# Leaving out the query columns of the first 10 or 14 tokens in eight attention-like heads

## The chip, the cores and the metric

The kernel runs on one core of one Trainium2 chip. The metric is device time in microseconds (us) of one execution; lower is better. TensorE (PE), VectorE (DVE), ScalarE (ACT), GpSimd (POOL) and SyncE (SP) each run their own list of instructions in order and wait for each other by semaphores.

## The reference, cut to what matters

The input is 1024 frames of 1024 features in float32; 16 learned meta tokens are put ahead of them (T = 1040 tokens). A token mixer with four mLSTM ("gated") heads and four retention heads is followed by a gated feed-forward network with a causal convolution over 3 tokens, and a final norm.

```
proj = up @ w_in                                   # up: normalised tokens
qk = silu(causal_dwconv(concat([ml_q, ml_k]), ml_conv_w))   # 4 taps, gated heads
rq = rotary(rt_q, pos); rk = rotary(rt_k, pos)              # retention heads
h = h + concat([gate(o) * head_norm(mlstm(q, k, v)), silu(g) * head_norm(retention(rq, rk, rv))]) @ w_out
h = h + channel_mixer(rmsnorm(h))     # its convolution takes the 2 tokens before each token
return rmsnorm(h)[:, 16:]             # the meta tokens are dropped at the end
```

Each token's query is used for that token's output alone. Only tokens 16 and later are returned, and the feed-forward convolution takes two tokens before them, so the mixer's output is needed from token 14 on. Keys and values of all tokens are needed, since they go into the running state.

## The kernel before, in words

Each matrix product in float32 is three TensorE products of rounded halves: high by high (L404), high by low (L405), low by high (L406). The queries and the keys of one head are a matrix of 128 rows (features) by 1040 columns (tokens), built in the three pieces of `PIECES`: columns 0 to 400, 400 to 784 and 784 to 1040. A piece is 8 blocks of the 1024 input features by three products, 24 matmuls, into one PSUM bank (`pq` for queries, `pk` for keys). `KEEP = 14` is the first token whose mixer output is needed; the output gate's first piece (`po`, 386 columns) starts there already, the query's starts at 0.

A piece is then taken out of PSUM. In a gated head (h = 0 to 3) DVE scales it (L425), copies three columns of overlap (L423), and runs the four taps of the convolution (L428 and three of L430) into `cvq` or `cvk`; ACT applies silu (L431) into `qT` or `kT`. In a retention head (h = 4 to 7) four DVE operations (L433 to L436) apply the rotary embedding and write `qT` or `kT`; ACT has no part in it. `qT` and `kT` are one tile each, used by all heads in turn.

The heads go in the order `ORDER = [4, 0, 1, 2, 3, 5, 6, 7]`. While one head's chunks are scanned (`scan_a`: scores `s` L816, weighted keys `kwh` on ACT L829; then the state update `u` on PE, L846), the matmuls of the next projections are laid between them. After a head's last chunk come its statistics (root L911 on ACT, L914 and L915 on DVE, the scaling L918 on ACT). `exps` (L555 to L559) makes the decay weights of a gated head: POOL adds a mask, ACT takes nine exponentials. `L808` and L809 split a scaled query into its halves on ACT and DVE. `L162` and L163 split weights into halves.

ACT holds one set of function tables at a time. Silu, sigmoid (L447), root and exponential change it, and the compiler puts an `ACT_TABLE_LOAD` before an activation that needs another set; it has the line of that activation. POOL also issues the accumulating DMAs of `w_out` (L212). The order of each engine's list comes from a scheduler of the framework, which runs a simulated timeline; so an edit may move instructions elsewhere.

Of the kernel before, what the change touches and what calls it, by code (L numbers as in the profile page):

```python
# [23 lines left out]
KEEP = 14  # L24
H = 4
# [38 lines left out]
def body(ctx, tc, h_in, vecs, cst, mask_in, rot, w_v0, w_v, w_fm, w_out, w_up, w_gate, w_down, out):  # L64
    nc = tc.nc
# [45 lines left out]
    def pp(name, tag="pp"):  # L111
        return ps.tile([P, 512], F32, tag=tag, name=name, bufs=PSB[tag])
# [58 lines left out]
    def need(key, ahead, loads=0):  # L171
        if not order:
            order.update({u[0]: i for i, u in enumerate(units)})
        issue(order[key] + 1 + ahead)
        if loads:
            load(order[key] + 1 + loads)
        return ready[key]
# [178 lines left out]
    qT = st.tile([P, T], F32, name="qT", tag="qT")  # L356
# [42 lines left out]
    def fm_mms(pt, U, t0, t1):  # L399
        hi, lo, _ = U  # L400
        n = t1 - t0
        for kb in range(KB):
            a, b = hi[:, kb * P:(kb + 1) * P], lo[:, kb * P:(kb + 1) * P]
            nc.tensor.matmul(pt[:, :n], a, uh[kb][:, t0:t1], start=kb == 0, stop=False)  # L404
            nc.tensor.matmul(pt[:, :n], a, ul[kb][:, t0:t1], start=False, stop=False)  # L405
            nc.tensor.matmul(pt[:, :n], b, uh[kb][:, t0:t1], start=False, stop=kb == KB - 1)  # L406
# [2 lines left out]

    def qk_group(h, kind, p):  # L410
        t0, t1, _ = PIECES[p]
        n = t1 - t0
        U = need((kind, h, 0), 2)
        pt = pp(f"p{kind}{h}_{p}")
        fm_mms(pt, U, t0, t1)
        dst = (qT if kind == "q" else kT)[:, t0:t1]
        raw = wk.tile([P, WMAX + 4], F32, tag="rawp", name=f"r{kind}{h}_{p}", bufs=2)
        if h < H:
            if p == 0:
                nc.vector.memset(raw[:, :3], 0.0)  # L420
            else:
                pr, pn = halo[kind]
                nc.vector.tensor_copy(raw[:, :3], pr[:, pn:pn + 3])  # L423
            halo[kind] = (raw, n)
            last["qk"] = nc.vector.tensor_tensor(raw[:, 3:3 + n], pt[:, :n], Rb[:, t0:t1], ALU.mult)  # L425
            w = V_CONV + ((0 if kind == "q" else H) + h) * 4
            cv = wk.tile([P, WMAX], F32, tag="cv", name=f"cv{kind}{h}_{p}", bufs=2)
            nc.vector.tensor_scalar(cv[:, :n], raw[:, 3:3 + n], vec[:, w + 3:w + 4], None, ALU.mult)  # L428
            for j in (2, 1, 0):
                nc.vector.scalar_tensor_tensor(cv[:, :n], raw[:, j:j + n], vec[:, w + j:w + j + 1], cv[:, :n], ALU.mult, ALU.add)  # L430
            last["silu"] = nc.scalar.activation(dst, cv[:, :n], AF.Silu)  # L431
        else:
            nc.vector.tensor_tensor(raw[0:64, :n], pt[64:128, :n], A2[64:128, t0:t1], ALU.mult)  # L433
            nc.vector.tensor_tensor(raw[64:128, :n], pt[0:64, :n], A2[0:64, t0:t1], ALU.mult)
            last["qk"] = nc.vector.tensor_tensor(dst, pt[:, :n], A1[:, t0:t1], ALU.mult)
            nc.vector.tensor_tensor(dst, dst, raw[:, :n], ALU.add)  # L436

    def o_group(h, b, p):
        t0, t1, _ = PIECES[p]
        t0 = max(t0, KEEP)  # L440
        n = t1 - t0
        U = need(("o", h, b), 4 if b and p and h not in (HF, 7) else 2)
        pt = pp(f"po{h}_{b}_{p}")
        fm_mms(pt, U, t0, t1)
        s = sig(b, p)
        nc.vector.tensor_tensor(s, pt[:, :n], Rb[:, t0:t1], ALU.mult)
        x = nc.scalar.activation(s, s, AF.Sigmoid if h < H else AF.Silu)  # L447
        if h < H:
            after(x, last["silu"])
        last["gate"] = x  # L450
# [564 lines left out]
    for kind in "qk":  # L1015
        for p in range(3):
            qk_group(HF, kind, p)
# [10 lines left out]
    for i, h in enumerate(ORDER):  # L1028
        A = lambda c, h=h: (lambda: scan_a(h, c))
        B = lambda c, h=h: ab(h, c)  # L1030
        merge([lambda b=b, p=p: (o_group(h, b, p), p == 1 and b and i and wsum_next()) for b in range(2) for p in range(3)],
              [A(0)] + [B(c) for c in range(4 if h < 7 else NCH)])
        if h == 7:
            break
        side = post_steps(h, 0) + [B(4), B(5), B(6)] + post_steps(h, 1) + [B(7), B(8)] + post_steps(h, 2)
        nxt = ORDER[i + 1]
        merge([lambda c=c: (v_group(nxt, c)(), c == 4 and i == 4 and wsum_next()) for c in range(NCH)], side)
        if i:
            tables(nxt)
        else:  # L1040
            exps(nxt)
        for kind in "qk":
            for p in range(3):
                qk_group(nxt, kind, p)
# [612 lines left out]
```

## Time and profile before

| what | value |
|---|---|
| time, median of 3 runs | 1535.11 us (1534.65 to 1535.12) |
| the profiled execution, its own time | 1536.01 us |
| its span, first to last instruction | 1534.2 us |
| mean granted TensorE clock | 0.997 of full speed |
| PE busy | 1516.1 us (99%) |
| DVE busy | 1094.6 us (71%) |
| ACT busy | 723.4 us (47%) |
| POOL busy | 101.5 us (7%) |

The profiled execution took 0.9 us more than the median of the runs, and 1.8 us of its time lie outside the span of instructions. A busy share is an average over the whole span; times of single instructions below are in us from the span's start.

### The profile page before, as it was taken

Reading aid. Unit: us, or ns where it says so; the run is one execution under the profiler, and the core shown is the slowest. Engines: PE = TensorE matmul, PEld = TensorE weight load, DVE = VectorE, ACT = ScalarE, POOL = GpSimd, SP = SyncE. Lnnn points to the kernel's source line nnn. Section 1 sums busy time; section 2 is a strip of 40 time slices with the busy share of each in tenths; the row PEclk is TensorE's granted clock in tenths of the full one; section 3 lists DMA queues with packets and bytes.
Section 4 is the critical chain, followed back from the end, with each engine's and each line's share of the span. In section 5 each row is a group of like instructions: output and inputs, shape, how many; then the busy total and the mean of one; then the engine's idle time right before and its main releaser. Section 6 shows DMA issues by size and latency. Waiting matters only on the chain.

```text
span 1534.2 us, 25396 instructions
## 1 busy us (share of the span) xinstructions
PE 1516.1 (99%) x9749; PEld 1392.2 (91%) x9749; DVE 1094.6 (71%) x2342; ACT 723.4 (47%) x1484; POOL 101.5 (7%) x120
## 2 busy tenths in 40 slices
PE   8999999999999999999999999999999999999997
PEld 7999999999999999997788998999999999888887
DVE  8767667676867575679968878667666666778657
ACT  7365554555542434335455455444444444344443
POOL 0000001010010000000000000211111010000000
PEclk9999999999999999999999999999999999999999
DMA  6123435352566334446443237888666667933313
GB/s 230 56 70 94 107 90 124 118 121 88 143 142 158 80 104 89 111 100 237 178 138 110 83 121 247 209 211 204 159 154 153 151 153 210 357 109 103 96 42 110
DMA packets 106232, 213.41 MB, mean 139 GB/s; under 512 B 10424, under 2 KB 32640, under 8 KB 106112
## 3 DMA queue, kind: packets, MB, share of 16 engines
q1 hardware_dynamic: 87424, 176.86, 34.8%
q0 software_dynamic: 18544, 34.87, 15.1%
q8 instruction: 76, 1.25, 0.3%
q14 instruction: 44, 0.36, 0.1%
q10 hardware_dynamic: 144, 0.07, 0.0%
HBM read 182.37 MB, written 84.19 MB: 174 GB/s over the span
## 4 chain that ended last, share of the span: by engine, by line
PE 97%; DVE 1%; ACT 1%; DMA 0%; issue 0%; DVEq 0%; ACTq 0%
PE pv L394 4%; PE pv L395 4%; PE pv L396 4%; PE po L404 4%; PE po L406 4%; PE po L405 4%; PE pdx L577 3%; PE pdx L579 3%; PE pdx L578 3%; PE pup_x L578 2%; PE pup_x L579 2%; PE pup_x L577 2%; PE pga_x L577 2%; PE pga_x L579 2%; PE pga_x L578 2%; PE pq L404 2%
## 5 line engine op out<-in xcount | busy, mean ns | idle before, releaser
L394 PE MATMUL pv<-hi_v,uh 128*128 128x256 f32 (+1 forms) x512 | 147.0, 288 | 2.6 <-ACT hi_v L162 1.6
L395 PE MATMUL pv<-lo_v,uh 128*128 128x256 f32 (+1 forms) x512 | 145.2, 284 | 0.0
L396 PE MATMUL pv<-hi_v,ul 128*128 128x256 f32 (+1 forms) x512 | 145.1, 284 | 0.0
L404 PE MATMUL po<-uh,hi_o 128*128 128x386 f32 (+2 forms) x384 | 124.0, 323 | 0.0
L405 PE MATMUL po<-ul,hi_o 128*128 128x386 f32 (+2 forms) x384 | 122.6, 319 | 0.0
L406 PE MATMUL po<-uh,lo_o 128*128 128x386 f32 (+2 forms) x384 | 122.6, 319 | 0.0
L394 PEld LDWEIGHTS pv<-hi_v,uh 128*128 128x128 f32 x512 | 97.3, 190 | 6.3 <-issue 2.9
L395 PEld LDWEIGHTS pv<-lo_v,uh 128*128 128x128 f32 x512 | 97.1, 190 | 0.9 <-DVE lo_v L163 0.8
L396 PEld LDWEIGHTS pv<-hi_v,ul 128*128 128x128 f32 x512 | 97.0, 190 | 0.0
L261 ACT CAST hi_up<-raw_up 128x512 fp32r<-128x512 f32 (+1 forms) x52 | 36.4, 719 | 110.0 <-PE pga_z L578 61.2
L212 POOL DMA_DIRECT2D wsd<-w_down_d x55 | 50.9, 1022 | 497.2 <-DMA wsd<-w_down_d 398.1
L404 PEld LDWEIGHTS po<-uh,hi_o 128*128 128x128 f32 x384 | 72.4, 189 | 0.2
L406 PEld LDWEIGHTS po<-uh,lo_o 128*128 128x128 f32 x384 | 72.3, 188 | 0.1
L405 PEld LDWEIGHTS po<-ul,hi_o 128*128 128x128 f32 x384 | 72.3, 188 | 0.1
L262 DVE TENSOR_TENSOR lo_ga<-fraw_ga,hi_ga 128x512 fp32r<-128x512 f32 (+1 forms) x52 | 41.9, 810 | 42.6 <-ACT hi_ga L261 42.5
L262 DVE TENSOR_TENSOR lo_up<-raw_up,hi_up 128x512 fp32r<-128x512 f32 (+1 forms) x52 | 41.4, 810 | 37.1 <-ACT hi_up L261 36.3
L577 PE MATMUL pup_x<-uh_g,hi_up 128*128 128x256 f32 (+1 forms) x240 | 67.3, 282 | 0.4 <-ACT uh_g L1061 0.4
L578 PE MATMUL pup_x<-ul_g,hi_up 128*128 128x256 f32 (+1 forms) x240 | 67.4, 282 | 0.1
L579 PE MATMUL pup_x<-uh_g,lo_up 128*128 128x256 f32 (+1 forms) x240 | 66.4, 282 | 0.0
L212 POOL DMA_DIRECT2D wsw<-w_out_d x40 | 37.2, 1028 | 398.7 <-DMA wsw<-w_out_d 361.4
L404 PE MATMUL pq<-uh,hi_q 128*128 128x400 f32 (+2 forms) x192 | 62.6, 326 | 0.2 <-DVE rq L425 0.2
L405 PE MATMUL pk<-ul,hi_k 128*128 128x400 f32 (+2 forms) x192 | 62.2, 324 | 0.0
(761 smaller groups left out, 5044.8 us busy)
## 6 DMA issues: line engine op xcount, KB each, us to landing
raw_up<-w_up_d SPq DMA_DIRECT2D x22, 512.0 KB, 5.6
fraw_ga<-w_gate_d SPq DMA_DIRECT2D x22, 512.0 KB, 3.7
acts<-cv SPq DMA_DIRECT2D x44, 256.0 KB, 6.1
wsd<-w_down_d SPq DMA_DIRECT2D x22, 512.0 KB, 6.8
wsd<-w_down_d POOLq DMA_DIRECT2D x22, 512.0 KB, 6.5
rd<-wsd SPq DMA_DIRECT2D x22, 512.0 KB, 3.6
wsd<-w_down_d POOLq DMA_DIRECT2D x33, 256.0 KB, 6.9
raw_o<-w_fm_d SPq DMA_DIRECT2D x16, 512.0 KB, 3.5
```

The costliest lines, as they stand in the source:

```text
L212: nc.gpsimd.dma_start(x, v, accum_op=ALU.add)
L261: nc.scalar.copy(hi[:, o:o + n], x)
L262: nc.vector.tensor_tensor(lo[:, o:o + n], x, hi[:, o:o + n].bitcast(F32), ALU.subtract)
L394: nc.tensor.matmul(pv[:L, :nv], a, hi[:, o:o + nv], start=kb == 0, stop=False)
L395: nc.tensor.matmul(pv[:L, :nv], a, lo[:, o:o + nv], start=False, stop=False)
L396: nc.tensor.matmul(pv[:L, :nv], b, hi[:, o:o + nv], start=False, stop=kb == KB - 1)
L404: nc.tensor.matmul(pt[:, :n], a, uh[kb][:, t0:t1], start=kb == 0, stop=False)
L405: nc.tensor.matmul(pt[:, :n], a, ul[kb][:, t0:t1], start=False, stop=False)
L406: nc.tensor.matmul(pt[:, :n], b, uh[kb][:, t0:t1], start=False, stop=kb == KB - 1)
L577: m.append(nc.tensor.matmul(pt, ah, xh_, start=first and k == 0, stop=False, skip_group_check=True))
L578: nc.tensor.matmul(pt, ah, xl_, start=False, stop=False, skip_group_check=True)
L579: m.append(nc.tensor.matmul(pt, al, xh_, start=False, stop=last and k == n - 1, skip_group_check=True))
```

## The change

In the first piece of the queries the product starts at column 10 in gated heads and at column 14 in retention heads. The columns before are no longer computed in any step of that piece (matmul, scaling, convolution, silu or rotary). One GpSimd copy for each head fills columns 0 to 10 (or 14) of `qT` from the columns that start at 14. A gated head keeps four columns more than are needed, of which the convolution reads three.

```
     def qk_group(h, kind, p):
         t0, t1, _ = PIECES[p]
+        cut = kind == "q" and p == 0
+        if cut:
+            t0 = KEEP - (4 if h < H else 0)
         n = t1 - t0
         U = need((kind, h, 0), 2)
         pt = pp(f"p{kind}{h}_{p}")
...
             last["qk"] = nc.vector.tensor_tensor(dst, pt[:, :n], A1[:, t0:t1], ALU.mult)
             nc.vector.tensor_tensor(dst, dst, raw[:, :n], ALU.add)
+        if cut:
+            nc.gpsimd.tensor_copy(qT[:, :t0], qT[:, KEEP:KEEP + t0])
```

In the changed file the lines of the projection's evacuation stand 3 further down (silu is L434), the copy is L441, and everything behind it is 5 further down (the root is L916, the split of a scaled query L813).

ACT, at the first query piece of head 1, before; `num` is the previous head's numerator, `cvq` the convolved query, `z` the statistics, `A` the decay weights:

```order
L880 COPY num_2_2682<-n_8_2732 128x257 [waits PE_49]
L431 ACT_TABLE_LOAD
L431 ACTIVATE qT<-cvq_0_2843 128x400 [waits DVE_49]
L911 ACT_TABLE_LOAD
L911 ACTIVATE z_2_2743<-z_2_2743 128x2 [waits DVE_49]
L559 ACT_TABLE_LOAD
```

The same place in the changed kernel:

```order
L885 COPY num_2_2684<-n_8_2734 128x257 [waits PE_49]
L434 ACT_TABLE_LOAD [waits DVE_49]
L434 ACTIVATE qT<-cvq_0_2845 128x390 [waits Pool_49]
L916 ACT_TABLE_LOAD
L916 ACTIVATE z_2_2745<-z_2_2745 128x2 [waits DVE_49]
L564 ACT_TABLE_LOAD
```

The order of the rows is the same. The silu now waits for POOL as well, since an earlier copy of POOL has read columns of `qT` that it overwrites, and the wait for DVE now stands on the table load ahead of it. Heads 0, 2 and 3 show the same.

PE, behind the last matmul of head 4's first query piece, before; `pra` and `pca` are small products for the norm factors of the tokens:

```order
L325 MATMUL pra_594<-cs,Rc 128x128 x2
L314 MATMUL pca_622<-cs,ssa_609 128x1 [waits Activation_49]
L314 MATMUL pca_622<-cs,ssa_609 128x1
L404 MATMUL pq_1_681<-uh_78,hi_q_0_399 128x384 [waits DVE_49]
L405 MATMUL pq_1_681<-ul_79,hi_q_0_399 128x384
```

In the changed kernel the same two products stand here:

```order
L404 MATMUL pq_1_682<-uh_80,hi_q_0_399 128x384
L405 MATMUL pq_1_682<-ul_81,hi_q_0_399 128x384
L314 MATMUL pca_622<-cs,ssa_609 128x1 [waits Activation_49]
L314 MATMUL pca_622<-cs,ssa_609 128x1
L406 MATMUL pq_1_682<-uh_80,lo_q_0_400 128x384
```

They have moved behind the first 11 matmuls of the second query piece.

DVE, at head 2's second query piece, before; `rq` is the scaled query, `qd` a query times its decay:

```order
L833 TENSOR_TENSOR qd_1_4207<-qT,A_190 128x128 [waits DMAHW4_49,Activation_49]
L425 TENSOR_TENSOR rq_1_3949<-pq_1_3924,Rb 128x384 [waits PE_49]
L914 RECIPROCAL z_2_3818<-z_2_3818 128x2 [waits Activation_49]
L428 TENSOR_SCALAR cvq_1_3952<-rq_1_3949,vec 128x384 [waits DVE_49]
L423 COPY rq_2_3983<-rq_1_3949 128x3
```

The same place in the changed kernel:

```order
L838 TENSOR_TENSOR qd_1_4211<-qT,A_190 128x128 [waits DMAHW4_49,Activation_49]
L919 RECIPROCAL z_2_3821<-z_2_3821 128x2 [waits Activation_49]
L428 TENSOR_TENSOR rq_1_3953<-pq_1_3928,Rb 128x384 [waits PE_49]
L920 SCALAR_TENSOR_TENSOR mv_2_3761<-mv_2_3761,z_2_3821 128x2 [waits DVE_49]
L431 TENSOR_SCALAR cvq_1_3956<-rq_1_3953,vec 128x384 [waits DVE_49]
```

The reciprocal, which waits for the root on ACT, now stands ahead of the scaling that empties the PSUM bank of the second piece. Heads 1 and 3 show the same.

## Rows read from the trace of the kernel before

**Rows 1.** The page: busy time by engine; the chain that ended last, by engine.

```profile
PE 1516.1 (99%) x9749; PEld 1392.2 (91%) x9749; DVE 1094.6 (71%) x2342; ACT 723.4 (47%) x1484; POOL 101.5 (7%) x120
...
PE 97%; DVE 1%; ACT 1%; DMA 0%; issue 0%; DVEq 0%; ACTq 0%
```

**Rows 2.** PE's waits: who waits for whom, us in total, times, longest.

```profile
PE pv L394 <- ACT hi_v L162: 1.6, 1, 1.6
...
PE pca L314 <- ACT Rb L329: 0.9, 2, 0.6
```

**Rows 3.** Timeline of PE, first query pieces: start, us, instruction, [idle before <- releaser].

```profile
39.17 0.34 PE L404 MATMUL pq<-uh,hi_q 128*128 128x400 f32 x1
...
42.80 0.34 PE L406 MATMUL pq<-uh,lo_q 128*128 128x400 f32 x1
...
46.69 0.34 PE L405 MATMUL pq<-ul,hi_q 128*128 128x384 f32 x1
...
50.54 0.34 PE L406 MATMUL pq<-uh,lo_q 128*128 128x384 f32 x1
```

**Rows 4.** Timeline of ACT, head 1, from the first query piece on.

```profile
220.76 1.28 ACT L431 ACT_TABLE_LOAD   x1
222.32 0.54 ACT L431 ACTIVATE qT<-cvq 128x400 f32<-128x400 f32 x1 [0.27 <-DVE cvq L430]
...
232.21 0.28 ACT L808 CAST qd_2h<-qd 128x128 fp32r<-128x128 f32 x1
...
247.66 0.42 ACT L431 ACTIVATE kT<-cvk 128x256 f32<-128x256 f32 x1 [0.39 <-DVE cvk L430]
248.08 1.28 ACT L447 ACT_TABLE_LOAD   x1
249.37 0.94 ACT L447 ACTIVATE sig<-sig 128x386 f32<-128x386 f32 x2
250.22 0.35 ACT L829 ACTIVATE kwh<-s,cols 128x128 fp32r<-128x128 f32 x1
```

**Rows 5.** Timeline of DVE, the same stretch.

```profile
221.65 0.63 DVE L430 SCALAR_TENSOR_TENSOR cvq<-rq,vec,cvq 128x400 f32<-128x400 f32 x1
...
228.56 0.29 DVE L809 TENSOR_TENSOR qd_1l<-qd,qd_1h 128x128 fp32r<-128x128 f32 x1 [1.44 <-ACT qd_1h L808]
...
232.52 0.29 DVE L809 TENSOR_TENSOR qd_2l<-qd,qd_2h 128x128 fp32r<-128x128 f32 x1 [0.40 <-ACT qd_2h L808]
...
247.13 0.48 DVE L430 SCALAR_TENSOR_TENSOR cvk<-rk,vec,cvk 128x256 f32<-128x256 f32 x1
```

**Rows 6.** Timeline of PE, head 1's first state update.

```profile
250.62 0.39 PE L846 MATMUL u<-vh,kwh 128*128 128x258 f32 x1
```

**Rows 7.** Timelines of ACT and PE, head 2.

```profile
334.37 0.35 ACT L829 ACTIVATE kwh<-s,cols 128x128 fp32r<-128x128 f32 x1
...
334.83 0.32 PE L846 MATMUL u<-vh,kwh 128*128 128x258 f32 x1
```

**Rows 8.** Timelines of ACT and PE, head 0.

```profile
133.55 1.28 ACT L431 ACT_TABLE_LOAD   x1
136.33 0.54 ACT L431 ACTIVATE qT<-cvq 128x400 f32<-128x400 f32 x1 [1.50 <-DVE cvq L430]
...
164.41 0.35 ACT L829 ACTIVATE kwh<-s,cols 128x128 fp32r<-128x128 f32 x1
...
168.44 0.28 PE L846 MATMUL u<-vh,kwh 128*128 128x258 f32 x1
```

**Rows 9.** Timeline of POOL.

```profile
88.15 0.22 POOL L555 TENSOR_TENSOR A<-A,mask 128x16 f32<-128x16 f32 x1 [86.52 <-DMA A<-scr]
...
212.95 2.40 POOL L556 TENSOR_TENSOR A<-A,mask 128x1024 f32<-128x1024 f32 x1 [41.51 <-DMA A<-scr]
238.36 1.06 POOL L212 DMA_DIRECT2D wsw<-w_out_d  x1 [23.01 <-DMA wsw<-w_out_d]
```

**Rows 10.** ACT's groups by line: count, busy us, mean ns of one, idle before.

```profile
L431 ACT ACT_TABLE_LOAD x8 | 10.3, 1283 | 0.1
```

More of the change, by code (lines that the diff above doesn't have):

```diff
@@ L411, in qk_group @@
         t0, t1, _ = PIECES[p]
+        cut = kind == "q" and p == 0
+        if cut:
+            t0 = KEEP - (4 if h < H else 0)
         n = t1 - t0
@@ L436, in qk_group @@
             nc.vector.tensor_tensor(dst, dst, raw[:, :n], ALU.add)
+        if cut:
+            nc.gpsimd.tensor_copy(qT[:, :t0], qT[:, KEEP:KEEP + t0])
     def o_group(h, b, p):
```

## The prediction

> **What bounds the kernel now.** I read the page first: PE is busy for 1516.1 us of the span and 97% of the chain that ended last [rows 1]. So a change gains what it takes out of PE's own work, and it costs whatever makes PE wait. The list of PE's waits comes next: the longest single one in the whole execution is 1.6 us, and none of the waits in the list is for `kwh` or for the score operands `qT` and `kT` [rows 2]. DVE (71%) and ACT (47%) just keep ahead. How far ahead they are at the places that the change touches decides the sign, so the timelines of the query pieces come last [rows 3 to 8].
>
> **Removed columns.** A first query piece has 24 matmuls. From start to start, 20 matmuls of 400 columns take 42.80 − 39.17 = 3.63 us, 181.5 ns each; 22 of 384 columns take 50.54 − 46.69 = 3.85 us, 175.0 ns each [rows 3]. That is 0.41 ns a column. Fourteen columns are worth 24 × 14 × 0.41 = 0.14 us in a retention head, ten are worth 0.10 us in a gated head: 4 × 0.14 + 4 × 0.10 = 0.96 us if PE never waits longer than now. Each DVE or ACT operation of the piece gets some 0.01 us shorter (the 390-column operation stands between rows of 0.57 us at 400 and 0.56 us at 384 columns; I take 5 × 0.01 = 0.05 us for the five of a convolved piece).
>
> **The copies.** No copy of this size on POOL is in the trace; the nearest row is an addition over 16 columns, 0.22 us [rows 9]. Below, nothing; above, the 2.40 us of the long mask addition [rows 9]. I take 0.2 us. Its reader is the first score matmul of the head's own scan, which stands just ahead of `kwh` at 250.22 and so over 20 us behind the silu at 222.32 [rows 4], and POOL has nothing to issue for long after it: in head 1 the mask addition is done at 215.4, the copy can run from about 223, and the next accumulating DMA starts at 238.36 [rows 9]. Even 2.40 us would be covered by these 15 us. If the cover were gone, the DMA would be late by 0.2 us a head. Cost: 0.
>
> **The new wait.** The silu of the first query piece overwrites columns that the copy of the head before has read. That copy runs one head earlier, 222.32 − 136.33 = 86 us by the silus [rows 4, 8], so waiting for POOL takes no time. But the order of ACT shows what it does to the rows: the table load in front of the silu had no wait, and in the changed kernel it carries the wait for DVE, while the silu carries that for POOL. Before, the load runs ahead while DVE is still at the convolution: in head 1 it goes from 220.76 to 222.04, then ACT idles for 0.27 us, and the silu starts at 222.32 [rows 4], 0.04 us after the last tap ends at 221.65 + 0.63 = 222.28 [rows 5]. Afterwards the load can only start when the tap is done: 0.04 + 1.28 us for a load (all eight of this line have a mean of 1283 ns [rows 10]) + 0.01 = 1.33 us behind the tap instead of 0.04. The silu is 1.29 us late, 1.24 us with the shorter DVE work.
>
> The Trainium skill states this splitting: instructions that wait for several engines may get event-semaphore instructions put ahead of them with the extra conditions (Perfetto Trace Analysis, Identifying Dependency Chains). The trace of before holds no such silu; by the page the wait goes ahead of the activation, and that it lands ahead of the table load too, only the order of the changed kernel shows.
>
> **Where the delay goes.** Heads 1, 2 and 3 have the same pattern. Behind the silu ACT is not idle until after 232.21 [rows 4]: a root, nine exponentials, scalings and splits with two more loads. DVE waits for ACT's splits at 228.56 (1.44 us) and 232.52 (0.40 us) [rows 5]: these waits are for ACT and so move with it; they absorb nothing. From there to 247.61 (247.13 + 0.48), DVE works through the key pieces without a wait in its timeline. Then ACT takes the last key silu at 247.66, 0.05 us behind DVE, a load at 248.08, the gate's sigmoids at 249.37, and `kwh` from 250.22 [rows 4], over at 250.57. PE's state update starts at 250.62 [rows 6]: 0.05 us of slack. A delay of 1.24 us at the silu therefore comes out on PE as 1.24 − 0.05 = 1.19 us. In head 2, `kwh` ends at 334.72 and PE reads it at 334.83 [rows 7]: 1.24 − 0.11 = 1.13 us. The third such head has the same margin as the second, within 0.02 us. The sum is 1.19 + 1.13 + 1.13 = 3.45 us. The 0.10 us that PE gains in each of these heads only makes its wait longer, since the chain through DVE and ACT sets the end; so it doesn't count.
>
> The swapped reciprocal on DVE waits for the root, and the scaling that empties the second piece's bank now comes behind it. The bank's next user is a key piece, with the third query piece's matmuls ahead of it: they are the cover, and the cost is 0. Without it PE would wait for the same lag of ACT earlier, which the later wait would then no longer hold: a shift of the stall, not an addition.
>
> **The other heads.** In head 0 the same load is held back, too: it ran from 133.55 and was followed by 1.50 us of idle time. But there `kwh` is over at 164.76, and the update starts at 168.44 [rows 8]: 3.7 us of slack, no wait, a gain of 0.10 us. Heads 5 to 7 write the queries on DVE, without a silu; the added wait there is for a copy long done: a gain of 3 × 0.14 = 0.42 us. In head 4, the first, the two small products move behind 11 matmuls. Before, they waited for ACT up to 0.6 us [rows 2]; this wait can vanish, or be taken over by the second piece, which now waits for the bank that DVE empties at about the same time, with the factors for the third piece later than before. I bound it by −0.6 us − 0.14 us below and +0.6 us above (the same wait once more, by the same row), and take +0.1 us, near the middle.
>
> **Sum.** 3.45 − 0.10 − 0.42 + 0.1 = +3.0 us. On the profiled execution's own 1536.01 us that is 1539.0 us; that execution is 0.9 us above the median of the runs, so I forecast 1535.1 + 3.0 = **1538.1 us**, about +0.20%. 0.2% of 1535.1 us is 3.1 us, about what a measurement of this kernel can tell from no change: the forecast stands on this border.
>
> **Rivals.** *A: the saving alone.* The wait on the load is there but something that I take for fixed (DVE's order of work between 232 and 248, where the timeline has many short rows) gives way, and PE never waits: −0.96 us, 1534.2 us. For it: PE has no wait for `kwh` now [rows 2]. Against it: the slack of 0.05 and 0.11 us [rows 4, 6, 7]. It decides if more than 1.1 us of hidden room lies in each head. This one ends on the other side, below before; it is also the outcome if the change does only what its lines say.
>
> *B: half of it is taken up,* for instance in two of three heads' key pieces: 1.2 to 1.7 us of stall less 0.4 us, about 1536.2 us.
>
> *C: the loads cost more than their bar.* The Trainium skill says that a switch of tables costs not only the load of about 1283 ns but also a drain, together about 2.66 us (ScalarE: Activation LUTs, What ACT_TABLE_LOAD costs). Worked out from rows as a mechanism here: if the silu came later behind a waiting load by as much again as the load, 1.28 us, in three heads, the time would be 3 × 1.28 = 3.8 us more, 1541.9 us. Against it: the load at 248.08 is followed by its activation at 249.37, 0.01 us after its end [rows 4]. By that page's figures the sum would be about 4.1 us more; the trace agrees with its 1283 ns and shows no drain. A milder way to the same side is head 4 at its upper bound of +0.6 us, or a second wait of 0.5 us a head behind the first, say at the transposes of the head before: 1539 to 1540 us.
>
> **How the numbers follow.** Forecast with three stalls: 0.70. Rival A 0.13, rival B 0.09, rival C with its milder form 0.08. The forecast's own range is 1537.2 to 1539.2 us: head 4 between −0.74 and +0.6 us instead of +0.1, and 0.1 us on each stall. To hold 8 in 10 the range has to take in A and B: 1533.9 to 1539.2 us. Slower by over 0.2% is above 1538.2: a little under half of the forecast's 0.70 (0.32) and C (0.08), 0.40. Faster by over 0.2% is below 1532.0, which no case reaches: 0.02. The rest, 0.58, is within 0.2%.
>
> **What would show it.** In the changed profile, the table load ahead of the first query silu in heads 0 to 3 starts right behind the last tap, and the silu 1.3 us after it; PE's waits list `kwh` (or the products that read it) with three waits of about 1.1 us; query matmuls of 386 and 390 columns have a pitch of 175 to 177 ns; POOL has eight copies of about 0.2 us and its DMAs no later than before. I am wrong if the load is early again, if PE shows no wait at the three state updates, if a retention head or head 0 gets a wait, or if the end of head 4's query pieces moves by more than 0.75 us.

## The result, and the profile after

The changed kernel takes 1540.37 us (median of 6 runs, 1540.12 to 1540.82); the kernel before, 1535.11 us in 6 runs. The ratio is 1.0033 with a 95% interval of 1.0023 to 1.0043: slower by 5.3 us, where +3.0 was forecast and 1539.2 was the upper end of the range. The profiled execution took 1540.17 us, with a span of 1538.1 us.

The page of the changed kernel, busy time and the chain by engine:

```profile
PE 1516.9 (99%) x9749; PEld 1390.8 (90%) x9749; DVE 1092.7 (71%) x2342; ACT 724.0 (47%) x1484; POOL 103.9 (7%) x128
...
PE 90%; DVE 4%; ACT 4%; issue 1%; DMA 0%; DVEq 0%; ACTq 0%
```

Set beside [rows 1], PE's count of matmuls is the same and its busy time nearly so (0.8 us more), but its part of the chain fell from 97% to 90%; DVE and ACT now have 4% each. The list of PE's waits says where:

```profile
PE u L851 <- ACT kwh L834: 2.1, 3, 0.7
...
PE pq L404 <- DVE qT L438: 0.8, 1, 0.8
...
PE tr L931 <- DVE sig L938: 0.5, 3, 0.2
...
PE pca L314 <- ACT Rb L329: 0.4, 1, 0.4
```

The first row was not there: three waits of 0.7 us for the weighted keys, one for each of heads 1 to 3. The third row is new as well: three waits, 0.5 us in all, at a transposition some 16 us ahead of the update. These rows show less than PE loses, since a wait in this list starts at the modelled end of the matmul before it, some 0.15 us after the next one could have started. In head 4 the wait for `Rb` ([rows 2]) got shorter, and a wait for DVE's query took its place.

Head 1, timeline of ACT; compare [rows 4]:

```profile
222.27 1.28 ACT L434 ACT_TABLE_LOAD   x1 [1.54 <-DVE cvq L433]
223.57 0.53 ACT L434 ACTIVATE qT<-cvq 128x390 f32<-128x390 f32 x1
...
249.32 1.28 ACT L452 ACT_TABLE_LOAD   x1
250.61 0.94 ACT L452 ACTIVATE sig<-sig 128x386 f32<-128x386 f32 x2
251.46 0.35 ACT L834 ACTIVATE kwh<-s,cols 128x128 fp32r<-128x128 f32 x1
```

The load sits idle for 1.54 us until the last tap is done, and starts 1.51 us later than before, though the taps end 0.09 us earlier. The silu is 1.25 us later, and `kwh` 1.24 us. Between them nothing is made up, as the timeline of DVE shows ([rows 5]):

```profile
221.57 0.62 DVE L433 SCALAR_TENSOR_TENSOR cvq<-rq,vec,cvq 128x390 f32<-128x390 f32 x1
...
224.13 0.29 DVE L838 TENSOR_TENSOR qd<-qT,A 128x128 f32<-128x128 f32 x1 [1.60 <-ACT qT L434]
225.65 0.17 DVE L919 RECIPROCAL z<-z 128x2 f32<-128x2 f32 x1 [1.22 <-ACT z L916]
...
248.38 0.48 DVE L433 SCALAR_TENSOR_TENSOR cvk<-rk,vec,cvk 128x256 f32<-128x256 f32 x1
```

The last tap of the keys starts at 248.38 instead of 247.13, 1.25 us later. PE in head 1:

```profile
250.20 0.42 PE L404 MATMUL po<-uh,hi_o 128*128 128x386 f32 x1
250.46 0.34 PE L405 MATMUL po<-ul,hi_o 128*128 128x386 f32 x1
250.64 0.34 PE L406 MATMUL po<-uh,lo_o 128*128 128x386 f32 x1
250.82 0.33 PE L404 MATMUL po<-uh,hi_o 128*128 128x386 f32 x1
251.86 0.39 PE L851 MATMUL u<-vh,kwh 128*128 128x258 f32 x1 [0.71 <-ACT kwh L834]
```

PE at the same place before, ahead of the update at 250.62 ([rows 6]):

```profile
249.59 0.42 PE L404 MATMUL po<-uh,hi_o 128*128 128x386 f32 x1
249.85 0.34 PE L405 MATMUL po<-ul,hi_o 128*128 128x386 f32 x1
250.03 0.34 PE L406 MATMUL po<-uh,lo_o 128*128 128x386 f32 x1
250.21 0.33 PE L404 MATMUL po<-uh,hi_o 128*128 128x386 f32 x1
250.38 0.33 PE L405 MATMUL po<-ul,hi_o 128*128 128x386 f32 x1
```

Four output-gate matmuls stand between the scores and the state update. Before there were five. The fifth now runs behind the update, after PE has waited. The prediction had missed this: it read the slack off the row of before ([rows 6]) and did not ask whether the update still stood at that place. The update itself is 1.24 us later than before. The transposition's wait takes a part of this first and adds nothing, since the end of `kwh` sets the update's time.

The first state update of head 3, before and in the changed kernel, shows what three heads add up to:

```profile
418.95 0.31 PE L846 MATMUL u<-vh,kwh 128*128 128x258 f32 x1
```

```profile
422.81 0.39 PE L851 MATMUL u<-vh,kwh 128*128 128x258 f32 x1 [0.72 <-ACT kwh L834]
```

It is 3.86 us later.

Head 0, ACT, and then PE ([rows 8]):

```profile
136.35 1.28 ACT L434 ACT_TABLE_LOAD   x1 [2.71 <-DVE cvq L433]
137.65 0.53 ACT L434 ACTIVATE qT<-cvq 128x390 f32<-128x390 f32 x1
...
164.84 0.35 ACT L834 ACTIVATE kwh<-s,cols 128x128 fp32r<-128x128 f32 x1
```

```profile
168.50 0.28 PE L851 MATMUL u<-vh,kwh 128*128 128x258 f32 x1
```

Here the load is just as late, `kwh` is over at 165.19, and PE comes to it 3.3 us afterwards: no wait.

The first query piece on PE ([rows 3]), and three of the eight copies on POOL:

```profile
39.19 0.34 PE L404 MATMUL pq<-uh,hi_q 128*128 128x386 f32 x1
...
42.73 0.34 PE L406 MATMUL pq<-uh,lo_q 128*128 128x386 f32 x1
...
46.14 0.44 PE L404 MATMUL pq<-uh,hi_q 128*128 128x384 f32 x1 [0.82 <-DVE qT L438]
```

```profile
46.83 0.20 POOL L441 COPY qT<-qT 128x14 f32<-128x14 f32 x1 [45.19 <-ACT vh L369]
...
224.16 0.32 POOL L441 COPY qT<-qT 128x10 f32<-128x10 f32 x1 [8.87 <-ACT qT L434]
...
646.30 0.71 POOL L441 COPY qT<-qT 128x14 f32<-128x14 f32 x1
```

Twenty matmuls of 386 columns take 3.54 us, 177 ns each: 24 × (181.5 − 177) = 0.11 us for a piece, not 0.14. The copies take 0.2 to 0.7 us, and the trace puts no engine's wait down to one of them.

### The profile page after: what moved, and what is told of

Read it like the earlier page. It is cut to its first block, busy times and chain, and to the rows that moved or that the text cites. A ratio compares the mean times of both kernels' runs of the same rounds, so it can differ in the third digit from the quotient of the medians.

```text
span 1538.1 us, 25422 instructions
## 1 busy us (share of the span) xinstructions
PE 1516.9 (99%) x9749; PEld 1390.8 (90%) x9749; DVE 1092.7 (71%) x2342; ACT 724.0 (47%) x1484; POOL 103.9 (7%) x128
## 3 DMA queue, kind: packets, MB, share of 16 engines
q8 instruction: 76, 1.25, 0.3%
## 4 chain that ended last, share of the span: by engine, by line
PE 90%; DVE 4%; ACT 4%; issue 1%; DMA 0%; DVEq 0%; ACTq 0%
PE pv L394 4%; PE pv L395 4%; PE pv L396 4%; PE po L406 3%; PE po L405 3%; PE po L404 3%; PE pdx L582 3%; PE pdx L584 3%; PE pdx L583 3%; PE pup_x L583 2%; PE pup_x L584 2%; PE pga_x L582 2%; PE pga_x L584 2%; PE pga_x L583 2%; PE pup_x L582 2%; PE pdy L582 2%
## 5 line engine op out<-in xcount | busy, mean ns | idle before, releaser
L404 PE MATMUL pq<-uh,hi_q 128*128 128x384 f32 (+3 forms) x192 | 62.3, 324 | 1.0 <-DVE qT L438 0.8
L406 PE MATMUL pk<-uh,lo_k 128*128 128x400 f32 (+2 forms) x192 | 62.3, 325 | 0.0
```

## The experiments

To see where time goes, I took matmuls by their place in PE's list and compared when they start in each trace with the first trace of before. A column is a place, headed by its start in that first trace; heads 1 to 3 lie between 216.2 and 424.1, heads 5 to 7 between 424.1 and 689.1. The last column is the loss in heads 1 to 3 (424.1 less 216.2).

```
us in first trace of before   38.7   50.9  216.2  424.1  689.1  700.0   1527  | heads 1-3
before_again                 +0.27  +0.29  +0.28  +0.08  +0.08  -1.02  -1.04  |  -0.20
before_third                 +0.49  +0.48  +0.46  +0.33  +0.33  +0.49  +0.49  |  -0.13
the change                   +0.01  +0.15  +0.03  +4.05  +3.76  +3.76  +3.72  |  +4.02
after_again                  +0.68  +0.82  +0.68  +4.83  +4.54  +3.42  +3.42  |  +4.15
after_third                  +0.58  +0.76  +0.64  +4.75  +4.46  +3.37  +3.28  |  +4.11
after_fourth                 -0.04  +0.11  -0.03  +3.94  +3.65  +3.66  +3.57  |  +3.97
gated_only                   -0.94  -0.96  -1.02  +2.95  +3.00  +3.01  +2.95  |  +3.97
wait_only                    -1.00  -1.02  -0.90  +2.97  +2.90  +2.89  +2.85  |  +3.87
order_5                      -0.23  -0.09  -0.30  +3.29  +2.95  +2.96  +2.85  |  +3.59
cover_12                     -1.28  -1.14  -1.28  +2.23  +1.86  +0.78  +0.71  |  +3.51
one_fill                     +0.37  +0.52  +0.40  +0.47  +0.18  -0.91  -0.94  |  +0.07
ret_only                     +0.44  +0.58  +0.55  +0.39  +0.05  -1.04  -1.15  |  -0.16
fill_preload                 +0.28  +0.42  +0.28  +0.04  -0.41  -1.52  -1.61  |  -0.24
preload                      +0.14  +0.64  +0.54  +0.17  -0.27  -1.39  -1.47  |  -0.37
act_copy                     -1.00  -0.86  -0.98  -1.41  -1.75  -2.85  -2.93  |  -0.43
```

The change and its three repeats are one program, as are the traces of before. The first 38.7 us differ by up to 0.7 us between executions of one program, and the step between 689 and 700 is either near 0 or −1.1 us. What lies between these repeats within 0.2 us. The first trace of before is the slowest of three in heads 1 to 3, so against their mean every loss in the last column is 0.1 us larger, and every gain 0.1 us smaller.

**Is it the wait, the copies or the columns?** Theory: the table load behind the wait. Rivals: the narrower pieces, and the copies or the wait for GpSimd in themselves. `wait_only` is before, plus

```
+        if kind == "q" and p == 0 and h < H:
+            nc.gpsimd.tensor_copy(spare, qT[:, KEEP:KEEP + 10])
```

> The kernel before with all 400 query columns computed, and only a GpSimd copy in each gated head, which reads ten columns of the queries into a tile of its own that nothing reads. Heads 1 to 3 get the same wait ahead of the table load as in the changed kernel; the order of PE's state updates is that of before. Theory (the late table load makes the stall): 3 x 1.29 less the slacks of 0.05, 0.11 and 0.13 is +3.6 us, about 1538.7 us. Rival (the narrower pieces or the columns themselves cost the time): within 0.3 us of before. Rival (the wait is worth all that the medians show and the saved columns too, 5.3 + 0.96): about 1541.3 us.

It took 1540.20 us, ratio 1.0035 (1.0023 to 1.0047), with 3.87 us lost in heads 1 to 3. ACT in head 1:

```profile
221.31 1.28 ACT L432 ACT_TABLE_LOAD   x1 [1.47 <-DVE cvq L431]
222.60 0.54 ACT L432 ACTIVATE qT<-cvq 128x400 f32<-128x400 f32 x1
```

No column is cut, nobody reads the copy, and the whole loss is there. PE waits 1.9 us for `kwh` in three places. The loss is a little over the 3.6 us worked out. The time alone would not decide, since it lies about halfway between the theory's 1538.7 and the last rival's 1541.3; the trace does.

`one_fill` is the change with one memset:

```
-        if cut:
-            nc.gpsimd.tensor_copy(qT[:, :t0], qT[:, KEEP:KEEP + t0])
+        if cut and h == HF:
+            nc.gpsimd.memset(qT[:, :t0], 0.0)
```

> The changed kernel, but the unread query columns are filled once, by a GpSimd memset in head 4, instead of by a copy in each head. The silu of heads 1 to 3 then waits for DVE alone, and its table load for nothing; the columns are cut as in the change; PE's state update stands one output-gate matmul earlier, as in the changed kernel. Theory: the saving of 0.96 us with at most 0.1 us of wait left in each of three heads, 1534.2 to 1534.6 us. Rival (the narrower pieces, or the moved state update, cost the time whatever the wait): 1538 to 1540 us. Rival (the copies' own work costs it): also 1534.2.

It took 1535.03 us, ratio 1.0000 (0.9991 to 1.0009), loss 0.07 us. ACT in head 1:

```profile
221.12 1.28 ACT L434 ACT_TABLE_LOAD   x1
222.65 0.53 ACT L434 ACTIVATE qT<-cvq 128x390 f32<-128x390 f32 x1 [0.25 <-DVE cvq L433]
```

The load runs ahead again and the loss is gone, with the columns cut and the state update at its new place. So the narrower pieces are not it, nor is the update's new place by itself, without the late load. Nor does the saving of the columns show in these heads, or in the time, which is 0.4 us above the range expected.

`preload` is the change with all its copies and waits, plus a silu of one column:

```
             nc.vector.tensor_scalar(cv[:, :n], raw[:, 3:3 + n], vec[:, w + 3:w + 4], None, ALU.mult)
+            if cut:
+                nc.scalar.activation(dum, cv[:, :1], AF.Silu)
```

> The changed kernel with all its copies and waits, and in each gated head one more silu over a single column, after the first tap of the convolution, whose result nothing reads; the table load goes with it, ahead of the waiting silu. Theory (the table load's place makes the stall, not the copy and not the wait for GpSimd): the stall goes, about 1534.4 us. Rival (the copies or the wait for GpSimd itself): as the changed kernel, 1539.3 to 1540.8 us.

It took 1534.82 us, ratio 0.9999 (0.9990 to 1.0008), and gained 0.37 us in heads 1 to 3. ACT in head 1:

```profile
216.68 1.28 ACT L434 ACT_TABLE_LOAD   x1
220.00 0.20 ACT L434 ACTIVATE dum<-cvq 128x1 f32<-128x1 f32 x1 [2.04 <-DVE cvq L432]
...
223.04 0.53 ACT L437 ACTIVATE qT<-cvq 128x390 f32<-128x390 f32 x1 [1.81 <-DVE z L915]
```

By the semaphores in its record the silu still waits for DVE and GpSimd; only its load is early. The state update stands behind the fifth matmul again here; behind the fourth, `one_fill` has hardly a loss either. So neither the copy nor the wait for GpSimd costs anything that can be seen; the place of the load does.

**Which heads?** The cut condition with `and h >= H` (retention heads alone) and with `and h < H` (gated heads alone):

> The changed kernel with columns cut and copies made in the four retention heads alone; the gated heads compute all 400 columns. Only head 0's silu then waits for GpSimd (for head 4's copy), and its table load comes late, where 3.7 us of slack lie behind it. Theory: no wait for kwh in any head, and a gain of 4 x 0.14 less what head 4's order costs: 1534.6 us, and -0.3 us on PE between 460 and 660 us. Rival (a late load costs its 1.3 us wherever it stands): 1535.8 us and a stop of PE in head 0.

> The changed kernel with columns cut and copies made in the four gated heads alone. Heads 1 to 3 wait as in the changed kernel, and PE's state update is one output-gate matmul early there. Theory: the whole loss without the retention heads' gain, 4.0 to 4.3 us on PE between 216 and 424 us and none behind, 1540.4 to 1541.4 us. Rival (the retention heads' copies have a part in the loss): under 3.5 us there.

`ret_only`: 1535.18 us, 0.9999 (0.9990 to 1.0007); between 424 and 689 us it gained 0.34 us. Its late load in head 0 (ACT, then PE):

```profile
136.92 1.28 ACT L434 ACT_TABLE_LOAD   x1 [2.85 <-DVE cvq L433]
138.21 0.54 ACT L434 ACTIVATE qT<-cvq 128x400 f32<-128x400 f32 x1
```

```profile
168.99 0.28 PE L851 MATMUL u<-vh,kwh 128*128 128x258 f32 x1
```

PE's update has no idle time ahead of it, so the late load, which has slack behind it, costs nothing there. The time is 0.6 us above the 1534.6 expected, and again it is the trace that decides. `gated_only`: 1540.04 us, 1.0029 (1.0018 to 1.0040), loss 3.97 us and nothing gained behind.

**The moved state update.** `order_5` is the change with the update held behind the fifth matmul, `cover_12` behind the twelfth (`ms` is the list of the piece's matmuls):

```
         ms = fm_mms(pt, U, t0, t1)
+        if 0 < h < H and b == 1 and p == 0:
+            after(last["u0"], ms[4])
```

> The changed kernel with one constraint on the order: in heads 1 to 3 PE's first state update follows the fifth output-gate matmul, where it stood before the change, instead of the fourth. The wait ahead of the table load stays. Theory (the moved update adds a matmul of 0.175 us to the stall in each head): the loss in heads 1 to 3 is 0.4 to 0.55 us smaller than in the changed kernel, 3.5 to 3.7 us instead of 4.0 to 4.15, and the wait for kwh 0.5 us each instead of 0.7. Rival (the place of the update is free, the table load is all): 4.0 to 4.15 us again.

> The same constraint with the twelfth output-gate matmul: PE has eight more matmuls, 1.4 us of work, ahead of the state update that waits. Theory (the stall is only a wait for kwh with nothing else left to do on PE): no wait for kwh, loss in heads 1 to 3 within 0.4 us of zero, time 1534.5 to 1535.8 us, with the late table loads still there. Rival (the lag of 1.2 us stays in the chain behind and comes out at the next step of the scan): 1.5 to 4 us of loss.

`order_5` took 1539.27 us, 1.0024 (1.0014 to 1.0034), loss 3.59 us, where the four traces of the change have 3.97 to 4.15. The mean of those is 4.06; so the moved update is worth 0.47 us, close to 3 × 0.175 = 0.53. That is one trace of `order_5`, and repeats differ by up to 0.2 us. PE in head 1:

```profile
250.62 0.33 PE L406 MATMUL po<-ul,hi_o 128*128 128x386 f32 x1
251.49 0.39 PE L883 MATMUL u<-vh,kwh 128*128 128x258 f32 x1 [0.54 <-ACT kwh L838]
```

`cover_12` was a miss: 1538.99 us, 1.0025 (1.0016 to 1.0033), loss 3.51 us. PE's waits, and its timeline in head 1:

```profile
PE n L855 <- ACT pt_0h L817: 1.8, 3, 0.6
```

```profile
250.61 0.29 PE L855 MATMUL n<-vh,pt_0h 128*16 128x258 f32 x1 [0.63 <-ACT pt_0h L817]
...
252.23 0.28 PE L883 MATMUL u<-vh,kwh 128*128 128x258 f32 x1
```

I had moved only the update. The numerator, whose operand ACT makes right behind `kwh`, came ahead of it and stopped PE in its place, after the same five matmuls. So the run says nothing on more cover. Its loss lies in the rival's range of 1.5 to 4 us, and in the way the rival had it: the lag belongs to ACT's list, and what reads from it next has to wait.

**Versions without the late load.** `act_copy` has `nc.scalar.copy` for the copy; `fill_preload` is `one_fill` with the one-column silu of `preload`.

> The changed kernel with the eight copies on ScalarE instead of GpSimd: the silu then waits for DVE alone and its table load for nothing; the copies of some 0.2 us stand in ACT's own list, and the state update behind the fifth output-gate matmul. Theory: no stall by a table load, but up to 0.2 us more of ACT in the chain ahead of kwh in heads 1 to 3, where the slack is 0.05 to 0.13 us: a loss of 0 to 0.4 us there, time 1534.5 to 1535.3 us. Rival (any copy behind the silu costs what the change does): 1539 to 1540 us.

> One memset in place of the eight copies, and the additional one-column silu that takes the table load early; PE's state update stands behind the fifth output-gate matmul. Theory: 0.3 us gained in heads 1 to 3, 0.3 in heads 5 to 7, 0.1 in head 0, 0.1 lost in head 4: about 0.6 us under before, 1534.5 us, too little to tell from no change in the times. Rival (the saved columns give nothing, since DVE and ACT set the pace there): within 0.1 us on PE between 216 and 424 us.

`act_copy`: 1533.96 us, 0.9993 (0.9984 to 1.0002). `fill_preload`: 1534.53 us, 0.9995 (0.9986 to 1.0003). Both times lie below before, by 1.0 and 0.5 us, and both intervals still hold no change. PE gains 0.43 and 0.24 us in heads 1 to 3 against the first trace of before; the two other traces of before have 0.20 and 0.13 themselves, so the second gain is not shown. ACT of `act_copy` in head 1:

```profile
219.73 1.28 ACT L434 ACT_TABLE_LOAD   x1
221.10 0.53 ACT L434 ACTIVATE qT<-cvq 128x390 f32<-128x390 f32 x1
...
227.02 0.18 ACT L441 COPY qT<-qT 128x10 f32<-128x10 f32 x1
```

The copy's 0.18 us behind the exponentials did not reach PE, against the 0 to 0.4 us that I had set for it.

**The rest between traces and medians.** Traces of the same two programs, and two kernels whose own work on PE is longer:

> The changed kernel once more, for its time beside the kernels of this group and for a second trace. If its two profiled executions are alike, PE's first state update of heads 1, 2 and 3 waits about 0.7 us each for kwh again, and PE's work stands about 1.4 us later behind each of these heads. Time 1539.3 to 1540.8 us.

> The kernel before as a run of its own, for a second trace. The first trace has 3.4 us at half clock at 693 to 697 us; traces of changed kernels without it are 1.1 us shorter there. If that stretch is chance, this trace may lack it: a span of about 1533.1 us instead of 1534.2. If it belongs to this kernel, it is there again. Time within 0.1% of before.

> The changed kernel, for a third trace. In heads 1 to 3 it should again lose 4.0 to 4.2 us against before, whatever the clock does elsewhere; half-clock stretches near 10, 36 and 697 us may be there or not, at about 0.4 to 1.1 us each. Time 1539.8 to 1541.0 us.

> The kernel before, for a third trace. If the stretch at half clock near 695 us belongs to stalled kernels, it is not there: a span of 1532.5 to 1533.3 us.

> The changed kernel, for a fourth trace. Loss in heads 1 to 3 of 4.0 to 4.2 us; the half-clock stretch near 697 us there or not, two of three so far without. Time 1539.8 to 1541 us.

> The kernel before with head 0's first query piece multiplied twice into the same bank: 24 more matmuls of 400 columns, 24 x 0.1815 = 4.36 us of PE's own work and no stop. If added work shows in the time one for one: 1539.3 to 1539.6 us. If a later arrival at the half-clock stretch costs 0.5 to 1 us in itself: 1540.0 to 1540.6 us.

> The same with head 3's first query piece, the last of the three heads that stall in the changed kernel; PE's state update of head 3 stands behind the fourth output-gate matmul here. One for one: 1539.3 to 1539.6 us; less if DVE and ACT catch up and PE had waits of its own, more as for pad_0 otherwise.

The padding is one more `fm_mms(pt, U, t0, t1)` in head 0 or 3. The change again: 1540.81, 1539.80 and 1540.20 us, ratios 1.0037, 1.0028 and 1.0032. Before again: 1535.07 and 1535.53 us, 0.9997 and 1.0001. The step between 689 and 700 us is a stretch at the lower clock, 1.2 instead of 2.4 GHz. Four traces, in windows of 2 us (the first trace of before, before_again, the change, after_again; the granted clock is the third number from the end):

```profile
694.00:696.00 2.00, 2.00 (x8) 1.77 (x9) 1.23 (x4) 1.97 (x3) 0.00 (x0) 0.50 1.02 379
```

```profile
694.00:696.00 2.00, 2.00 (x13) 1.74 (x12) 1.94 (x4) 1.97 (x4) 0.00 (x0) 1.00 1.05 396
```

```profile
698.00:700.00 2.00, 2.00 (x9) 1.78 (x9) 0.91 (x3) 1.97 (x4) 0.00 (x0) 0.53 1.04 399
```

```profile
698.00:700.00 2.00, 2.00 (x13) 1.67 (x12) 1.93 (x6) 1.98 (x3) 0.00 (x0) 1.00 1.04 387
```

With the same program it is there or not: in two of three traces of before and two of four of the change. So it is no part of the change, and `before_third`, which had it, was a miss. `pad_0` came out 3.4 us longer in the medians and 3.4 us longer on PE between 39 and 689 us (4.4 were worked out; by its PE places a part of the added work is made up within head 0, and what gave way there I did not find). `pad_3` is 5.4 us longer in the medians (five runs) and 4.8 us on PE; it also has a wait of 0.3 us for `kwh` in head 1, so it is not added work alone. Time that PE loses thus shows one for one in `pad_0`, where a later arrival at that stretch costs nothing by itself. In `pad_3` the median moves 0.6 us more than PE does, as in the changed kernel, so what a later arrival costs stays open for these.

## Why the prediction was wrong

The mechanism held. Two steps failed: the slack, a term of the sum, and the way from a trace to the median. The forecast was 2.3 us short. Of this, 0.6 us are the slack, 0.5 us smaller terms, and 1.1 us the second step.

- *The new wait.* Right. The load starts behind the last tap, the silu 1.25 us late (1.24 forecast). The Trainium skill gives a drain besides the load, about as long as the load itself (ScalarE: Activation LUTs, What ACT_TABLE_LOAD costs). This trace does not agree: after the load at 222.27 the silu starts at 223.57, 0.02 us behind its end. Rival C's doubled delay is not there.
- *Where the delay goes.* The chain was right, the term of the sum mis-sized: 3.45 us forecast, 3.97 to 4.15 measured, and 4.1 to 4.35 against the other two traces of before. The step that failed is the slack: "1.24 − 0.05" took the state update to be where it stood in before. The order of the changed kernel has it one matmul earlier in heads 1 to 3, so PE reaches the wait 0.175 us sooner and does that matmul afterwards. Head 3's update shows both parts. Of its 3.86 us, 0.03 are older than head 1, and 2 × 0.175 = 0.35 are the matmuls done behind the updates of heads 1 and 2. The other 3.48 us are the lateness of `kwh` in three heads, close to the 3.45 forecast. Less the 0.03 and with the third moved matmul, the three heads lose 4.0 us, as in the table. With the update at its old place, 3.59 us are lost.
- *The sign to look for.* PE's list was to show three waits of about 1.1 us for `kwh`; it shows 0.7. The moved matmul, the wait at the transposition and the way the list counts make the difference. The second wait that was a rival's milder form came, but did not add to the loss.
- *Removed columns.* 0.96 us was too much: the pitch at 386 columns is 177 ns, where 0.41 ns a column gives 175.8. Heads 5 to 7 gained 0.29 us in each of four traces (0.42 forecast), head 0 0.12 to 0.14 us (0.10).
- *Head 4.* +0.14 to +0.18 us, taken as +0.1. The wait for `Rb` became one for the bank, as feared.
- *Copies and DMAs.* Free, as forecast; a copy took up to 0.71 us instead of 0.2.
- *Sum.* 0.14 − 0.12 + 4.02 − 0.29 to 689 us, and 0.15 us behind, is +3.9 us of span for the profiled pair (1538.1 − 1534.2), against +3.0.
- *From the trace to the median.* This is the second step that failed. The forecast set +3.0 on a median of 1535.1, with 0.1 us for each stall and no part for what differs from execution to execution. (By these terms its own range is 1537.0 to 1538.9, not 1537.2 to 1539.2.) The two profiled executions differ by 1540.17 − 1536.01 = 4.16 us: 3.9 in the span, and 0.26 outside it, a part that the forecast took to be the same. With 4.16 the forecast would have been 1539.3, just over its upper end. The remaining 1.1 us are the distance of these two executions from their medians: that of before lies 0.9 us above, that of the change 0.2 below. The forecast let both executions lie 0.9 us above their medians.
- *What stays open.* All 25 runs of the changed kernel have a median of 1540.1 us, 5.0 above before's 1535.16 (129 runs). Of this, 3.9 us are on PE between 39 and 689 us (four traces of the change against three of before), 0.15 behind 700 us, and 0.3 outside the span. The other 0.6 us is not settled. The first 39 us move by up to 0.7 us and the stretch near 697 us by 1.1 us between executions of one program, and seven traces do not say how often.

## What to carry to other kernels

An instruction of another engine that reads or fills columns of a shared tile can give the next writer of these columns a second wait, even if it was over long ago. Where the writer needs new function tables, look at which wait the compiler puts on the load: if the load was running ahead of its data, it may stop doing so, as here. Fill such a corner once, or on the engine that writes the tile; and when a slack is read off a row of before, check in the new order that the waiting instruction still stands there.

## What was not expected of the hardware

In one program, executed again and again, PE's granted clock goes to 0.50 for about 3.4 us at changing places: near 697 us in four of the seven traces of before and the change, near 36 us in the other three, and near 10 us in two of these. Near 697 us it costs 1.1 us. This makes single executions of one program differ by more than the work that this change was to save.
